# Pre-norm gain: from broadcast rows to the transposed rows, and a reordered start, in a two-layer decoder trunk

## The chip, the cores and the metric

The kernel runs on one core of a Trainium2 chip. The metric is the device time of one execution in microseconds, as the median over runs; lower is better. A core has five engines with an instruction queue each, which run in parallel and meet at semaphores: TensorE (PE in the profile; its weight loads are PEld), VectorE (DVE), ScalarE (ACT), GpSimd (POOL) and SyncE (SP), which here only issues transfers. Matmul results go to PSUM, all other tiles lie in SBUF.

## The reference

Two layers work on 512 tokens of 1024 channels. Each layer normalises x, projects it at once to 3488 columns for four head groups (low-rank attention, a gated convolution, a spatial gate, block-sparse attention), gates and concatenates their outputs, projects them back, and adds the residual. What the change touches is the first line of a layer and the first columns of the projection:

```python
def rmsnorm(x, g):
    xf = x.astype(jnp.float32)
    y = xf * lax.rsqrt(jnp.mean(xf * xf, axis=-1, keepdims=True) + EPS)
    return (y * g).astype(x.dtype)
...
    h = rmsnorm(x, norm_g)
    p = h @ w_in
    ...
    q = (rmsnorm(cq, mla_q_norm_g) @ mla_w_uq).reshape(B, S, MLA_HEADS, MLA_QK)
    kv = (rmsnorm(ckv, mla_kv_norm_g) @ mla_w_ukv).reshape(B, S, MLA_HEADS, MLA_NOPE + MLA_V)
```

## The kernel before, in words

**Tiles.** The 512 tokens are four tiles (t = 0 to 3) of 128 rows, the 1024 channels eight blocks (kt, or "k block") of 128. A float32 product is made of three matmuls of rounded values: each operand is split into hi (rounded to the matmul's type, fp32r) and lo (the rest, also fp32r), and hi·hi, hi·lo and lo·hi are summed in PSUM. `split2` makes such a pair out of a tile: ScalarE writes hi, then VectorE writes lo = source - hi.

**Pre-norm of one tile** (`pre_norm`). ScalarE squares both halves of x and sums them (`square_half`, into `xss`); POOL adds the two sums and the epsilon and takes the power -1/2 (`pow_rstd`). VectorE writes h in two halves of 512 columns, each x times the row's scalar times the gain g, where g is a row that was broadcast to all 128 partitions (`L.ng`). PE transposes each half in a group of four 128x128 blocks into one PSUM slot (`trS`, two slots, shared with cT and others); the profile calls the slot hT, and cT where the low-rank rows are transposed. One ScalarE instruction of 512 columns then writes hi (`hTh`), one of VectorE lo (`hTl`), and the slot is free.

**Where g comes from.** In layer 0 a row of g is loaded into a zeroed tile (`gz`), and two matmuls with a matrix of ones copy it to all partitions (`ng` in the profile). In layer 1 two transfers broadcast it from memory (`load_norm_gain`).

**The first stage of a layer** (`main`, `tok`). For each tile PE makes cq: eight k blocks, three matmuls of 416 columns each, from the weight units c0 to c3 (two blocks each). Then `low_chain` multiplies by the low-rank gains (ct), transposes (cT, three blocks), splits (cTh, cTl), and makes q (six matmuls of 384 columns) and kv (three of 512); `low_stats`, `q_chain` and `kv_chain` make the statistics and Q, K and Vt of the head groups. Their scalars (ms, mq, mk) are powers taken on POOL, and krt, Q and K on VectorE wait for them. The weight units are loaded by SP into raw tiles (`raw_...`) and split by `split_units`, half a unit at a time, into `whi_...` on ScalarE or VectorE and `wlo_...` on VectorE; the first units of the next product, sq, are split early, into `yTh` and `yTl`. The rope tables are about 60 small operations, most of them on POOL.

**What sets the order.** The program is written by an order of its own: each piece of work is a Python generator with a modelled time for every engine (`Order`, `Chain`), and instructions are emitted when the model says that they are due. What is emitted stays in that order on each engine, so each queue is fixed at build time, and an instruction that waits holds up all that is behind it on its engine. `ROPET` and `MIXT` are modelled times at which the rope tables and the parameter work may begin; `L0.par_t` is one for the low-rank chains; `NWARM` and `NWARM2` count matmuls on ones that run ahead of the work; `LOAD_HOOKS` say behind which weight unit a tile of x is loaded.

Of the kernel before, what the change touches and what calls it, by code (L numbers as in the profile page):

```python
# [11 lines left out]
F32 = mybir.dt.float32  # L12
F32R = mybir.dt.float32r
I32 = mybir.dt.int32
AF = mybir.ActivationFunctionType
ALU = mybir.AluOpType
AX = mybir.AxisListType

P = 128
# [15 lines left out]
NWARM, NWARM2 = 3, 1  # L35
ROPET, MIXT = 7000.0, 23000.0
# [160 lines left out]
def hybrid_trunk(ctx: ExitStack, tc: tile.TileContext, x, positions, norm_g, w_c, w_f, w_t, w_o, mla_q_norm_g,  # L197
# [180 lines left out]
    maskb = cst.tile([P, S], F32, name="maskb")  # L378
    cosT = cst.tile([P, NT, 16], F32, name="cosT")
# [94 lines left out]
    def load_norm_gain(L):  # L474
        ch = Chain(o)
        L.ng = []
        for c in (0, 512):
            g = yield from t2S.get(ch, f"ng{c}_{L.l}")
            dma(ch, P * 2048, g, dram(norm_g, L.l * D + c, [[0, P], [1, 512]]))
            L.ng.append(g)  # L480
        o.set(L.ng_ev, ch.t)

# [28 lines left out]
    for l in range(DEPTH):  # L511
        L = Layer()
        L.l = l
        L.ng_ev = Event()
        L.hT = [[Event(), Event()] for _ in range(NT)]
# [28 lines left out]
    def pre_norm(L, t, xx, t0, release):  # L544
        ch = Chain(o, t0)
        s1 = L.xss[t]
        yield from ch.pool(G.tensor_scalar, s1[:, 2:3], s1[:, 0:1], s1[:, 1:2], EPS, op0=ALU.add, op1=ALU.add)
        yield from pow_rstd(ch, s1[:, 3:4], s1[:, 2:3], 1)
        yield from ch.wait(L.ng_ev)
# [3 lines left out]
        for c in range(2):  # L553
            sl = slice(c * 512, (c + 1) * 512)
            yield from ch.dve(V.scalar_tensor_tensor, h[:, sl], in0=xx[:, sl], scalar=s1[:, 3:4], in1=L.ng[c],
                              op0=ALU.mult, op1=ALU.mult)
            tps.append(ch.t)
        release(ch)
        if t == NT - 1:
            for _ in range(2):  # L560
                (t2S if L.l else sS).put(ch)

        def half(c):
            c2 = Chain(o, tps[c])
            tp = yield from trS.get(c2, f"hT{t}_{c}_{L.l}")
            for k in range(4):
# [3 lines left out]
            yield from split2(c2, hTh[:, c * 4:c * 4 + 4, t * P:(t + 1) * P],  # L570
                              hTl[:, c * 4:c * 4 + 4, t * P:(t + 1) * P], tp.rearrange("p (k n) -> p k n", k=4))
            trS.put(c2)
            o.set(L.hT[t][c], c2.t)
# [592 lines left out]
    def main():  # L1166
        m = Chain(o)

        def tok(L, n, width, t, dst, us):

            for k in range(KT):
                if n == "c" and k % 4 == 0:
                    yield from m.wait(L.hT[t][k // 4])
# [14 lines left out]
        for L in layers:  # L1188
# [40 lines left out]
            for half in range(2):  # L1229
# [17 lines left out]
                for group, cut in (((0, 1, 2), YCUT), ((3,), 0)) if half == 0 else (((t,), 0) for t in range(NT)):  # L1247
# [16 lines left out]
                    if half == 0 and group[0] == 0 and l + 1 < DEPTH:  # L1264
                        o.spawn(load_norm_gain(layers[l + 1]))
# [9 lines left out]
    def start():  # L1275
        cw = Chain(o)
        ones = (yield from zzS.get(cw, "ones"))
        gz = yield from hS.get(cw, "gz")
        yield from cw.dve_fast(V.memset, ones[:, 0:256], 1.0)
        yield from cw.dve_fast(V.memset, gz, 0.0)  # L1280
# [4 lines left out]
        L0.ng = []  # L1285
        for c in range(2):
            L0.ng.append((yield from sS.get(cg, f"ng{c}")))
# [95 lines left out]
```

## Time and profile before

| | |
|---|---|
| median of 3 runs | 508.67 us (508.65 to 508.96) |
| the profiled execution | 508.65 us |
| its span | 506.8 us (1.85 us lie around it) |
| TensorE busy | 498.1 us, 98% |
| VectorE busy | 349.3 us, 69% |
| ScalarE busy | 296.5 us, 58% |
| GpSimd busy | 139.2 us, 27% |
| mean granted TensorE clock | 0.996 |

A row of a timeline gives start and duration in microseconds, engine, line of the kernel, operation, output<-inputs by the program's names, shape and count, and in brackets the idle time of the engine just before it with the instruction that ended it. A row of a group gives the total busy time in microseconds, the mean of one in nanoseconds, and the engine's idle time before it. Nearly all instructions go through one helper line (L158, and L184 on PE), so they are told apart by the names of the tiles. Durations overlap: an engine may start an instruction before the one ahead has ended.

### The profile page before, as it was taken

How to read it: one execution, taken by the hardware profiler on the slowest of the kernel's cores; microseconds unless marked ns; L12 is line 12 of the kernel's file. 1: busy time of each engine (PE TensorE's matmuls, PEld its weight loads, DVE VectorE, ACT ScalarE, POOL GpSimd, SP SyncE). 2: the span in 40 equal slices, each digit the busy share in tenths (PEclk: the TensorE clock that was granted, in tenths of full speed). 3: DMA queues.
4: the chain of work that ended last, by engine and by line, in shares of the span. 5: the costliest groups of instructions: out<-in, count | busy, mean ns of one | idle time of the engine just before them, and what ended most of it. 6: DMA issues, size and time to landing. Idle time of an engine off the chain costs nothing.

```text
span 506.8 us, 7665 instructions
## 1 busy us (share of the span) xinstructions
PE 498.1 (98%) x2508; PEld 423.3 (84%) x2508; DVE 349.3 (69%) x917; ACT 296.5 (58%) x891; POOL 139.2 (27%) x321
## 2 busy tenths in 40 slices
PE   6999999999999999999999999999999999999997
PEld 4898888888888888888889988888888888888886
DVE  4877975468799887635576988777868887635311
ACT  5698764567687775424247894677766777432100
POOL 6867875452000000000121488513330000000000
PEclk9999999999999999999999999999999999999999
DMA  8533415112114123464443242140142121624111
GB/s 273 165 123 114 125 43 166 41 43 66 60 43 166 52 74 109 142 175 117 143 155 126 83 125 71 55 124 2 42 167 82 43 83 49 201 84 164 66 54 50
DMA packets 20618, 51.57 MB, mean 102 GB/s; under 512 B 5985, under 2 KB 7265, under 8 KB 20578
## 3 DMA queue, kind: packets, MB, share of 16 engines
q1 hardware_dynamic: 20546, 51.08, 31.1%
q8 instruction: 20, 0.33, 0.3%
q0 software_dynamic: 32, 0.00, 0.1%
q14 instruction: 20, 0.16, 0.1%
HBM read 46.87 MB, written 4.19 MB: 101 GB/s over the span
## 4 chain that ended last, share of the span: by engine, by line
PE 90%; POOL 4%; DVE 2%; DMA 2%; ACT 1%; issue 1%; POOLq 0%; DVEq 0%
PE o L184 17%; PE kv L184 10%; PE cq L184 6%; PE sq L184 5%; PE cc L184 4%; PE gb L184 4%; PE cb L184 4%; PE gd L184 4%; PE gc L184 4%; PE ch L184 4%; PE su L184 4%; PE sa L184 3%; PE ga L184 3%; PE oa L184 2%; PE od L184 2%; PE sd L184 2%
## 5 line engine op out<-in xcount | busy, mean ns | idle before, releaser
L158 DVE TENSOR_TENSOR xr<-o,xr 128x512 f32<-128x512 f32 (+1 forms) x17 | 11.2, 658 | 42.0 <-PE o L184 42.0
L184 PE MATMUL o<-whi_wo,yTl 128*128 128x512 f32 (+1 forms) x102 | 38.4, 377 | 0.0
L184 PE MATMUL o<-wlo_wo,yTh 128*128 128x512 f32 (+1 forms) x102 | 38.4, 377 | 0.0
L184 PE MATMUL o<-whi_wo,yTh 128*128 128x512 f32 (+1 forms) x102 | 38.4, 376 | 0.0
L158 ACT ACTIVATE whi_wo<-raw_wo 128x512 fp32r<-128x512 f32 x31 | 18.3, 624 | 21.7 <-PE o L184 13.6
L158 ACT ACTIVATE pa<-pa,mna 128x256 f32<-128x256 f32 (+3 forms) x44 | 23.4, 539 | 5.2 <-DVE mna L158 5.1
L184 PE MATMUL kv<-whi_kv,hTh 128*128 128x512 f32 x64 | 26.0, 406 | 0.0
L184 PE MATMUL o<-whi_wo,yD 128*128 128x512 f32 (+1 forms) x68 | 25.7, 381 | 0.0
L158 ACT ACTIVATE pd<-pd,mnd 128x256 f32<-128x256 f32 (+3 forms) x46 | 24.5, 546 | 2.0 <-DVE mnd L158 1.5
L158 ACT ACTIVATE pha<-pTa 128x512 fp32r<-128x512 f32 (+3 forms) x32 | 13.9, 434 | 20.1 <-PE pTa L184 19.9
L184 PE MATMUL kv<-whi_kv,hTl 128*128 128x512 f32 x64 | 25.1, 392 | 0.0
L184 PE MATMUL kv<-wlo_kv,hTh 128*128 128x512 f32 x64 | 24.9, 390 | 0.0
L158 ACT ACTIVATE phd<-pTd 128x512 fp32r<-128x512 f32 (+3 forms) x32 | 13.9, 435 | 18.4 <-PE pTd L184 18.3
L184 PE MATMUL cq<-whi_c,hTh 128*128 128x416 f32 x64 | 24.3, 380 | 0.0
L184 PE MATMUL cq<-whi_c,hTl 128*128 128x416 f32 x64 | 23.3, 365 | 0.0
L184 PE MATMUL cq<-wlo_c,hTh 128*128 128x416 f32 x64 | 23.0, 360 | 0.0
L158 DVE TENSOR_TENSOR wlo_wo<-raw_wo,whi_wo 128x512 fp32r<-128x512 f32 x32 | 21.0, 687 | 2.4 <-ACT whi_wo L158 2.0
L184 PEld LDWEIGHTS o<-wlo_wo,yTh 128*128 128x128 f32 x102 | 19.2, 188 | 3.6
L184 PEld LDWEIGHTS o<-whi_wo,yTh 128*128 128x128 f32 x102 | 19.2, 188 | 3.6
L184 PEld LDWEIGHTS o<-whi_wo,yTl 128*128 128x128 f32 x102 | 19.2, 188 | 3.5
L158 DVE CUSTOM_DVE_ANT_0 pa<-sa,maskb 128x512 f32<-128x512 f32 (+3 forms) x32 | 15.0, 485 | 8.7 <-PE pTa L184 4.6
L158 DVE TENSOR_TENSOR pld<-pTd,phd 128x512 fp32r<-128x512 f32 (+3 forms) x32 | 15.5, 486 | 4.9 <-ACT phd L158 4.8
(328 smaller groups left out, 1712.8 us busy)
## 6 DMA issues: line engine op xcount, KB each, us to landing
raw_wo<-in_w_o_dram SPq DMA_DIRECT2D x16, 512.0 KB, 3.9
raw_sq<-in_w_t_dram SPq DMA_DIRECT2D x8, 512.0 KB, 3.5
raw_kv<-in_w_t_dram SPq DMA_DIRECT2D x8, 512.0 KB, 3.5
raw_c<-in_w_c_dram SPq DMA_DIRECT2D x8, 416.0 KB, 4.2
raw_ga<-in_w_f_dram SPq DMA_DIRECT2D x4, 512.0 KB, 3.6
raw_su<-in_w_f_dram SPq DMA_DIRECT2D x4, 512.0 KB, 3.5
raw_gc<-in_w_f_dram SPq DMA_DIRECT2D x4, 512.0 KB, 3.6
raw_ch<-in_w_f_dram SPq DMA_DIRECT2D x4, 512.0 KB, 3.4
```

The costliest lines, as they stand in the source:

```text
L158: f(*a, **k)
L184: f(*a, **k)
```

## The change

The gain is no longer multiplied into h. It is loaded once for both layers as 16 rows of 128 (a row for each layer and k block), transposed by PE to `gT`, in which column kt has the gain of that block's 128 channels, one per partition. h is x times the row's scalar alone (a `tensor_scalar`). After the transposes, where channels lie on partitions, hi and lo of each 128x128 block are formed with that column as a per-partition scalar: four ScalarE and four VectorE instructions of 128 columns for each half, in place of one and one of 512. PE waits for each k block (`L.hT[t][k]`), and the PSUM slot is given back after the fourth lo. `gz` with its memset, the two broadcast matmuls and the two broadcast loads of layer 1 go.

At the start, tile 0's x is loaded as 640 and 384 columns (`X0CUT`) in place of two halves; VectorE squares and sums the first part with one instruction that also adds the epsilon, ScalarE the second. Six warm-up matmuls stand ahead and none behind. x1 is loaded behind c1 and not behind c0. The rope tables are due at 13000 instead of 7000, the parameter work at 21000 instead of 23000, the low-rank chains at 15500 instead of 17500. The order of all queues in the first 45 us follows from these.

```diff
@@ -32,8 +32,8 @@
 NRAW, NW, NT2 = 2, 6, 9
 WSLACK = 0.0
 AHEAD = 4
-NWARM, NWARM2 = 3, 1
-ROPET, MIXT = 7000.0, 23000.0
+NWARM, X0CUT = 6, 640
+ROPET, MIXT = 13000.0, 21000.0
 ROPEB, ROPEV = 400.0, 200.0
 EARLY = ('sq0', 'sq1', 'sq2')
 YORDER, YCUT = (2, 3, 0, 1, 4, 6, 5, 7), 6
@@ -376,6 +376,7 @@
     ident = cst.tile([P, P], F32, name="ident")
     make_identity(nc, ident)
     maskb = cst.tile([P, S], F32, name="maskb")
+    gT = cst.tile([P, DEPTH * KT], F32, name="gT")
     cosT = cst.tile([P, NT, 16], F32, name="cosT")
     sinT = cst.tile([P, NT, 16], F32, name="sinT")
     hTh = big.tile([P, KT, S], F32R, name="hTh")
@@ -471,15 +472,6 @@
     class Layer:
         pass
 
-    def load_norm_gain(L):
-        ch = Chain(o)
-        L.ng = []
-        for c in (0, 512):
-            g = yield from t2S.get(ch, f"ng{c}_{L.l}")
-            dma(ch, P * 2048, g, dram(norm_g, L.l * D + c, [[0, P], [1, 512]]))
-            L.ng.append(g)
-        o.set(L.ng_ev, ch.t)
-
     def load_params(L):
         l = L.l
         L.cg = lay.tile([P, 384], F32, tag="cg_b", name="cg_b")
@@ -511,8 +503,7 @@
     for l in range(DEPTH):
         L = Layer()
         L.l = l
-        L.ng_ev = Event()
-        L.hT = [[Event(), Event()] for _ in range(NT)]
+        L.hT = [[Event() for _ in range(KT)] for _ in range(NT)]
         L.xss = [cst.tile([P, 4], F32, name=f"xss{t}_{l}") for t in range(NT)]
         L.qd = [Event() for _ in range(NT)]
         L.kd = [Event() for _ in range(NT)]
@@ -542,23 +533,22 @@
                           accum_out=L.xss[t][:, c:c + 1])
 
     def pre_norm(L, t, xx, t0, release):
+
         ch = Chain(o, t0)
         s1 = L.xss[t]
-        yield from ch.pool(G.tensor_scalar, s1[:, 2:3], s1[:, 0:1], s1[:, 1:2], EPS, op0=ALU.add, op1=ALU.add)
+        if L.l == 0 and t == 0:
+            yield from ch.pool(G.tensor_tensor, s1[:, 2:3], s1[:, 0:1], s1[:, 1:2], op=ALU.add)
+        else:
+            yield from ch.pool(G.tensor_scalar, s1[:, 2:3], s1[:, 0:1], s1[:, 1:2], EPS, op0=ALU.add, op1=ALU.add)
         yield from pow_rstd(ch, s1[:, 3:4], s1[:, 2:3], 1)
-        yield from ch.wait(L.ng_ev)
         h = yield from hS.get(ch, f"h{t}_{L.l}")
         hput = shared(hS, 2)
         tps = []
         for c in range(2):
             sl = slice(c * 512, (c + 1) * 512)
-            yield from ch.dve(V.scalar_tensor_tensor, h[:, sl], in0=xx[:, sl], scalar=s1[:, 3:4], in1=L.ng[c],
-                              op0=ALU.mult, op1=ALU.mult)
+            yield from ch.dve_fast(V.tensor_scalar, h[:, sl], xx[:, sl], s1[:, 3:4], None, op0=ALU.mult)
             tps.append(ch.t)
         release(ch)
-        if t == NT - 1:
-            for _ in range(2):
-                (t2S if L.l else sS).put(ch)
 
         def half(c):
             c2 = Chain(o, tps[c])
@@ -567,10 +557,17 @@
                 kt = c * 4 + k
                 yield from c2.pe(109.0, PE.transpose, tp[:, k * P:(k + 1) * P], h[:, kt * P:(kt + 1) * P], ident)
             hput(c2)
-            yield from split2(c2, hTh[:, c * 4:c * 4 + 4, t * P:(t + 1) * P],
-                              hTl[:, c * 4:c * 4 + 4, t * P:(t + 1) * P], tp.rearrange("p (k n) -> p k n", k=4))
-            trS.put(c2)
-            o.set(L.hT[t][c], c2.t)
+            ca, cv = Chain(o, c2.t), Chain(o, c2.t)
+            for k in range(4):
+                kt = c * 4 + k
+                src, g = tp[:, k * P:(k + 1) * P], gT[:, L.l * KT + kt:L.l * KT + kt + 1]
+                hi, lo = (z[:, kt, t * P:(t + 1) * P] for z in (hTh, hTl))
+                yield from ca.act(A.activation, hi, src, AF.Copy, scale=g)
+                cv.t = max(cv.t, ca.t)
+                yield from cv.dve(V.scalar_tensor_tensor, lo, in0=src, scalar=g, in1=hi.bitcast(F32), op0=ALU.mult,
+                                  op1=ALU.subtract)
+                o.set(L.hT[t][kt], cv.t)
+            trS.put(cv)
         for c in range(2):
             o.spawn(half(c))
 
@@ -1169,8 +1166,8 @@
         def tok(L, n, width, t, dst, us):
 
             for k in range(KT):
-                if n == "c" and k % 4 == 0:
-                    yield from m.wait(L.hT[t][k // 4])
+                if n == "c":
+                    yield from m.wait(L.hT[t][k])
                 if t == 0 and k % 2 == 0:
                     us.append((yield from unit(m, f"{n}{k // 2}_{L.l}")))
                 wh, wlo = us[k // 2]
@@ -1262,7 +1259,6 @@
                             if i1 == KT:
                                 o.spawn(out_chain(L, half, t, acc[t], o.now + PELAT))
                     if half == 0 and group[0] == 0 and l + 1 < DEPTH:
-                        o.spawn(load_norm_gain(layers[l + 1]))
                         load_params(layers[l + 1])
             early_put(m)
             ydS.put(m)
@@ -1275,22 +1271,18 @@
     def start():
         cw = Chain(o)
         ones = (yield from zzS.get(cw, "ones"))
-        gz = yield from hS.get(cw, "gz")
+        gn = ones[0:DEPTH * KT, 256:384]
         yield from cw.dve_fast(V.memset, ones[:, 0:256], 1.0)
-        yield from cw.dve_fast(V.memset, gz, 0.0)
         wp = yield from accS.get(cw, "warm")
         for _ in range(NWARM):
             PE.matmul(wp[:, 0:256], ones[:, 0:P], ones[:, 0:256], start=True, stop=True)
         cg = Chain(o)
-        L0.ng = []
-        for c in range(2):
-            L0.ng.append((yield from sS.get(cg, f"ng{c}")))
         x0 = yield from v4S.get(cg, "x0_0", [P, D], F32)
         L0.x[0] = x0
-        for c in range(2):
-            dma(cg, P * 2048, x0[:, c * 512:(c + 1) * 512], x[0, 0:P, c * 512:(c + 1) * 512])
+        for c, sl in enumerate((slice(0, X0CUT), slice(X0CUT, D))):
+            dma(cg, P * 4 * (sl.stop - sl.start), x0[:, sl], x[0, 0:P, sl])
             o.set(L0.x0[c], cg.t)
-        nc.sync.dma_start(gz[0:1, :], dram(norm_g, 0, [[D, 1], [1, D]]))
+        nc.sync.dma_start(gn, dram(norm_g, 0, [[P, DEPTH * KT], [1, P]]))
 
         def after(t):
             def f():
@@ -1298,10 +1290,10 @@
             return f
         for n in ("c0_0", "c1_0"):
             units[n].wanted = True
-        LOAD_HOOKS["c0_0"] = (after(1),)
+        LOAD_HOOKS["c1_0"] = (after(1),)
         LOAD_HOOKS["c3_0"] = (after(2), after(3))
         LOAD_HOOKS["ukv_0"] = (lambda: load_params(L0),)
-        L0.par_t = 17500.0
+        L0.par_t = 15500.0
         o.spawn(load_units(), None, 4)
         o.spawn(split_units(), None, 5)
         o.spawn(rope_tables(), ROPET, 6)
@@ -1309,24 +1301,29 @@
         for t in range(NT):
             def pre(t):
                 ch = Chain(o)
-                h = None
-                for c in range(2):
-                    yield from ch.wait(L0.x0[c] if t == 0 else L0.xr[t])
-                    if c == 0:
-                        h = yield from sS.get(ch, f"sq{t}")
-                    yield from square_half(ch, L0, t, c, h, L0.x[t])
+                sq = yield from sS.get(ch, f"sq{t}")
+                if t == 0:
+                    yield from ch.wait(L0.x0[0])
+                    xa, xb, s1 = x0[:, 0:X0CUT], x0[:, X0CUT:D], L0.xss[0]
+                    jk = yield from hS.get(ch, "sqj")
+                    yield from ch.dve(V.tensor_tensor_reduce, out=jk[:, 0:X0CUT], in0=xa, in1=xa, scale=1.0 / D,
+                                      scalar=EPS, op0=ALU.mult, op1=ALU.add, accum_out=s1[:, 0:1])
+                    hS.put(ch)
+                    ch = Chain(o, L0.x0[1].t)
+                    yield from ch.act(A.activation, sq[:, 0:D - X0CUT], xb, AF.Square, scale=D ** -0.5,
+                                      accum_out=s1[:, 1:2])
+                else:
+                    yield from ch.wait(L0.xr[t])
+                    for c in range(2):
+                        yield from square_half(ch, L0, t, c, sq, L0.x[t])
                 sS.put(ch)
                 yield from pre_norm(L0, t, L0.x[t], ch.t, v4S.put)
             o.spawn(pre(t), None, 0 if t == 0 else 6)
-        for c in range(2):
-            ch = Chain(o, 4000.0)
-            yield from ch.pe(860.0, PE.matmul, L0.ng[c], ones[:, 0:P], gz[:, c * 512:(c + 1) * 512], start=True, stop=True)
-        for _ in range(NWARM2):
-            PE.matmul(wp[:, 0:256], ones[:, 0:P], ones[:, 0:256], start=True, stop=True)
+        ch = Chain(o, 4000.0)
+        yield from ch.pe(60.0, PE.transpose, wp[:, 256:256 + DEPTH * KT], gn, ident[0:DEPTH * KT, 0:DEPTH * KT])
+        yield from ch.dve(V.tensor_copy, gT, wp[:, 256:256 + DEPTH * KT])
         accS.put(ch)
         zzS.put(ch)
-        hS.put(ch)
-        o.set(L0.ng_ev, ch.t)
 
     o.spawn(start())
     o.run()
```

## The prediction

> **What bounds the kernel now.** I read the page's head, then the windows by stage, the waits, the timeline of the first 40 us, and the groups by form for prices.
>
> ```profile
> span 506.8 us, 7665 instructions
> PE 498.1 (98%) x2508; PEld 423.3 (84%) x2508; DVE 349.3 (69%) x917; ACT 296.5 (58%) x891; POOL 139.2 (27%) x321
> PE   6999999999999999999999999999999999999997
> PE 90%; POOL 4%; DVE 2%; DMA 2%; ACT 1%; issue 1%; POOLq 0%; DVEq 0%
> ```
>
> TensorE (PE) is busy in every slice but the first and the last, and 90% of the chain that ended last. The stages are told apart by windows (busy time and count for PE, PEld, DVE, ACT, POOL; then granted clock):
>
> ```profile
> core 0: us, PE busy (x) PEld busy (x) DVE busy (x) ACT busy (x) POOL busy (x), PEclk, DMA share, GB/s
> 0.00:11.05 11.05, 6.51 (x19) 3.87 (x20) 4.42 (x9) 4.85 (x10) 7.34 (x36) 1.00 0.78 251
> 11.05:15.10 4.05, 4.05 (x15) 3.58 (x14) 3.57 (x7) 3.65 (x10) 3.54 (x8) 0.58 1.03 407
> 15.10:40.00 24.90, 24.30 (x141) 22.91 (x141) 20.00 (x48) 19.72 (x72) 18.89 (x38) 1.00 0.41 123
> ...
> 60.00:500.00 440.00, 439.95 (x2220) 372.97 (x2220) 303.68 (x793) 250.65 (x715) 93.81 (x219) 1.00 0.29 95
> ```
>
> From 15 to 500 us PE idles 0.6 us. So only the start can give time back, at most the few us before TensorE is dense, while any later wait of PE is a pure loss. From 15 to 40 us VectorE (DVE) is busy 20.0 of 24.9 us and PE hardly waits: there VectorE is close behind, and the change adds to it there.
>
> ```profile
> PE hT L184 <- DVE h L158: 3.0, 2, 2.6
> ```
>
> **The change, part by part.** *The start.* Rows of before:
>
> ```profile
> 1.36 0.91 DVE L158 MEMSET gz<- 128x1024 f32 x1 [0.16 <-issue]
> 4.42 2.10 PE L184 MATMUL ng<-gz,ones 128*128 128x512 f32 x4 [0.24 <-DMA gz<-in_norm_g_dram]
> 7.78 0.39 DVE L158 CAST whi_c<-raw_c 128x416 fp32r<-128x416 f32 x1 [5.50 <-DMA raw_c<-in_w_c_dram]
> 9.51 0.66 PE L184 MATMUL hT<-ident,h 128*128 128x128 f32 x4 [2.55 <-DVE h L158]
> ```
>
> The memset of gz goes, and with it the wait of the norm-gain load on SP ahead of raw_c0: raw_c0 may land up to 0.9 earlier, 6.9 to 7.8; I take 7.6, near the row, since the transfers ahead of it are the same. The two broadcast matmuls (2.1 us) and a warm-up go, three warm-ups and one 16-row transpose of g come; all lie in PE time that waits for h: nothing. One copy of g (16 columns) and the first tile's square of 640 columns on VectorE lie before raw_c0, where VectorE idles 5.50: nothing. The layer-1 gain loads leave SP in the dense part: nothing. x1 is issued behind c1 instead of ahead of it; its pre-norm stands behind weight splits on VectorE anyway.
>
> What the start then costs is VectorE's queue, in the built order, at these prices:
>
> ```profile
> L158 DVE TENSOR_TENSOR hTl<-hT,hTh 128x512 fp32r<-128x512 f32 x16 | 10.9, 684 | 5.0 <-ACT hTh L158 5.0
> L158 DVE SCALAR_TENSOR_TENSOR h<-x,xss,ng 128x512 f32<-128x512 f32 x8 | 5.9, 742 | 2.2 <-POOL xss L158 2.2
> L158 DVE TENSOR_TENSOR wlo_c<-raw_c,whi_c 128x416 fp32r<-128x416 f32 x16 | 9.1, 596 | 1.6 <-ACT whi_c L158 1.6
> L158 DVE TENSOR_TENSOR yTl<-raw_sq,yTh 128x512 fp32r<-128x512 f32 x12 | 8.3, 689 | 2.0 <-ACT yTh L158 1.9
> L158 DVE TENSOR_SCALAR pa<-pa,mna 128x512 f32<-128x512 f32 x8 | 3.9, 484 | 0.1
> L158 DVE SCALAR_TENSOR_TENSOR Vt<-kv,ms,Vt 128x256 fp32r<-128x256 f32 x8 | 3.8, 477 | 0.8 <-ACT Vt L158 0.8
> L158 DVE TENSOR_TENSOR Mt<-kv,Mt 128x256 fp32r<-128x256 f32 x8 | 3.4, 422 | 3.9 <-ACT Mt L158 3.9
> L158 DVE TENSOR_TENSOR pld<-pTd,phd 128x128 fp32r<-128x128 f32 x8 | 2.3, 286 | 0.8 <-ACT phd L158 0.8
> L158 DVE SCALAR_TENSOR_TENSOR Q<-Q,mq,gq_b 128x96 f32<-128x96 f32 x32 | 10.0, 313 | 0.5 <-POOL mq L158 0.5
> L158 DVE CAST whi_sq<-raw_sq 128x512 fp32r<-128x512 f32 x2 | 0.8, 423 | 0.0
> L158 ACT ACTIVATE phd<-pTd 128x128 fp32r<-128x128 f32 x8 | 2.2, 269 | 3.1 <-PE pTd L184 3.1
> ```
>
> A half of h falls from 742 ns to that of a scalar multiply, 484. A lo of 128 columns: 286 without a per-partition scalar (pld); the scalar adds 477 − 422 = 55 (Vt against Mt), so 344, and four of them take the place of one of 684. Back to back, starts are closer than durations:
>
> ```profile
> 22.17 0.74 DVE L158 SCALAR_TENSOR_TENSOR h<-x,xss,ng 128x512 f32<-128x512 f32 x1
> 22.83 0.42 DVE L158 TENSOR_TENSOR wlo_ukv<-raw_ukv,whi_ukv 128x256 fp32r<-128x256 f32 x1
> 23.17 0.55 DVE L158 TENSOR_TENSOR cTl<-cT,cTh 128x384 fp32r<-128x384 f32 x1
> ```
>
> that is, duration less 0.08. So a half costs 0.40 + 4 × 0.265 = 1.46 instead of 0.66 + 0.60 = 1.26. From raw_c0's landing to tile 1's last lo the queue holds 7 halves of h (2.8), 16 lo's (4.2), 8 wlo_c (4.1), four casts at 0.3 (1.2), four operations of 384 columns (1.9) and two wlo_ukv (0.7): 14.9. With 0.5 for waits, an estimate, tile 1's last lo ends at 7.6 + 14.9 + 0.5 = 23.0; cTl, just ahead of it, at 22.75.
>
> By the Trainium skill, "VectorE: DVE Perf Modes", section "The TRN2 errata — SBUF-src ops pay a fixed extra latency per instruction", cost is a fixed part per instruction plus the columns, so small tiles lose: it speaks against four for one, and the rows agree (286 for 128 columns, 684 for 512). Its figure for a PSUM source, 120 cycles plus the columns at 0.96 GHz, would make a lo 258 ns; by it the total would be about 2.0 lower (23 × 0.086).
>
> *Tile 2.* Rows at which before's PE passes the same work:
>
> ```profile
> 28.79 0.60 PE L184 MATMUL hT<-ident,h 128*128 128x128 f32 x4
> 29.15 0.44 PE L184 MATMUL cq<-whi_c,hTh 128*128 128x416 f32 x1
> ...
> 35.95 0.35 PE L184 MATMUL cq<-whi_c,hTh 128*128 128x416 f32 x1
> ```
>
> A group of four transposes takes 0.36. The 6.80 between the two cq rows (tile 2's and tile 3's fourth k block) hold 24 cq, 6 q, 3 kv and one group: 6.44 / 33 = 0.195 a matmul. In the built order both transpose groups of tile 2 stand on PE behind q0's four last matmuls, which need cTl, and kv0's three: the first group starts at 22.75 + 7 × 0.195 = 24.1 and ends 0.6 later, and the first hi on ScalarE takes about 0.35 (phd's 269 and a scalar's fetch): 25.1. VectorE comes to tile 2's first lo at 23.0 + 0.4 (h) + 0.2 (ms) = 23.6 and waits 1.5, with everything behind it. Then up to the first half's fourth lo stand 7 lo's (1.9; the halves are interleaved), three yTl (1.8), two 512-column casts (0.7), wsl (0.6, as yTl), ct (0.5), Vt (0.4), krt and ms (0.3): 6.2, end at 31.3. PE, from 22.75, has 19 matmuls (3.7) and two groups (0.7) until then, and is free at 27.2. Next stands tile 3's first transpose group. Two PSUM slots serve all of them, and a slot is now held until its half's fourth lo, not until one lo: the group can't go before 31.3 either, and the fourth k block starts at 31.3 + 0.36 = 31.7. Before starts it at 29.15, less cT1 (three transposes, about 0.25), which the new order has later: 28.9. So here the kernel is 31.7 − 28.9 = **2.8 late**.
>
> *Tile 3.* From there to its fourth lo: eight lo's (2.1), three yTl (1.8), three Q (0.7), ct 0.5, ms, mq, mk 0.6, krt and K 0.4: 6.1, end at 37.4. Before is there at 35.95, less q1 and kv1, which now come later (9 × 0.195 = 1.75): 34.2. So **3.2 late**, 0.4 more. After it the rest of tile 3 has PE's q1, kv1 and q2 between, so VectorE catches up.
>
> *POOL.* The rope tables start behind tile 1's gain instead of at once:
>
> ```profile
> 11.22 0.19 ACT L158 ACTIVATION_READ_ACCUMULATOR sq<-x 128x1 f32 x1
> ...
> 7.30 0.19 POOL L158 CAST posf<-posi 128x4 f32<-128x4 int32 x1 [1.30 <-DMA posi<-in_positions_dram]
> ...
> 26.08 0.72 POOL L158 TENSOR_TENSOR ms<-ms,nhalf 128x2 f32<-128x2 f32 x1
> ```
> ```profile
> L158 POOL TENSOR_SCALAR rope_scratch<-rope_scratch 128x64 f32<-128x64 f32 x30 | 14.3, 478 | 2.3
> L158 POOL TENSOR_TENSOR rope_scratch<-rope_scratch 128x64 f32<-128x64 f32 x22 | 9.4, 425 | 1.4
> L158 POOL TENSOR_TENSOR mq<-mq,nhalf 128x4 f32<-128x4 f32 x8 | 8.7, 1082 | 12.7 <-DVE mq L158 10.1 <-DVE ms L158 2.7
> ```
>
> Before has x1's squares at 11.4; behind one more load of 416 KB (1.05 at the 407 GB/s of the second window) and with the gain's sum and pow (about 1.0) posf comes at 13.4. To the pow of ms stand 10 and 4 rope operations of 64 columns (0.57 and 0.5 with a gap of 0.09), four short ones (1.8), tile 2's and 3's gains and three small jobs: 14.9, so 28.3; krt on VectorE asks at about 27.2. Then 7 and 6 rope operations and the pow of mq: 36.4; the first Q on VectorE asks at 33.7, and 3.9 of its queue follow to tile 3's fourth lo, 40.3 instead of 37.4. So POOL costs 0 (where its operations run quicker or VectorE asks later than I have it) to 2.9, by the groups' means; POOL's durations spread widely, and I take the middle, **1.4**.
>
> *Layer 1.* The same split, with room:
>
> ```profile
> 248.66 0.68 DVE L158 TENSOR_TENSOR hTl<-hT,hTh 128x512 fp32r<-128x512 f32 x1
> ...
> 260.36 0.43 PE L184 MATMUL cq<-whi_c,hTh 128*128 128x416 f32 x1
> ```
>
> Tile 0's last lo is 11 us ahead of its use: nothing; without that cover 0.2 a half. ScalarE's four hi's for one cost it about 0.4 a half; it is 79% busy at the start and its work runs ahead of VectorE's.
>
> Sum: 508.65 + 3.2 + 1.4 = 513.3 (506.8 of span and 1.85 around it, which stays). The profiled execution took 508.65, the median of the runs is 508.67: the same.
>
> **The rivals.** *Faster:* PE doesn't wait. VectorE keeps ahead as it does in 15–40 us of before, and what is left is the earlier start: PE free at 27.2 where before is at 28.55 (28.9 without that group): −1.3, 507.35. It decides if tile 2's fourth lo ends 4.1 earlier than I have it. For it: VectorE has 4.9 us idle in that window. Against: 1.5 of wait for transposes and yTl, wsl and casts in front. *No difference:* that lo at 28.5, and POOL in time: 508.65. *POOL never late:* 511.9. *POOL wholly late:* 514.8. *The clock:* PE would idle 4.1 us between 25 and 31.3. In before, its wait of 2.55 (row at 9.51) is followed by 4.05 us at a granted 0.58: 3.4 at half rate, 1.7 lost. Were that to come again: 515.0. By the Trainium skill, "TensorE: Matmul & The Clock Gate", section "Part 1: The HAM clock gate", an idle window of about 3.4 us halves the rate until a busy window has passed; the 3.4 us of before agree. Against it, the new idle time is cut by matmuls.
>
> **How the numbers follow.** Chances: forecast 0.25, POOL never late 0.24, wholly late 0.20, clock 0.10, faster 0.15, no difference 0.06. Without the scalar's 55 ns a lo, 23 lo's are 1.3 cheaper (512.0); with half of Vt's 477 and a full gap, 0.40 each, 3.1 dearer (516.4). The likeliest one's own range is 511.9 to 514.8; the range is 508.0 to 516.4, which leaves out "faster" and a little above. A measurement tells 0.2% from no change, 1.0 us: faster 0.15, same 0.06, slower 0.79.
>
> **What would show it.** Of the changed kernel: tile 1's last hTl near 23, the first hTl of tile 2 near 25 with VectorE idle before it (released by ScalarE's hTh), PE waiting for DVE hTl between 25 and 38 for some 4 us, POOL's pow of ms after krt's turn, hTl at 344 and h at 484, the windows from 60 us on unchanged, and VectorE over 90% busy from 7.6 to 23. If PE shows no wait in 25–40, I am wrong in the queue's length; if it waits longer, in POOL or in the clock.

## The result, and the profile after

The changed kernel takes 520.21 us (median of 4 runs, 519.78 to 520.74); the kernel before takes 508.81 in the same comparison. The ratio is 1.0221, with a 95% interval of 1.0203 to 1.0239: 11.4 us slower. The forecast was slower, at 513.3 in a range up to 516.4: the sign is right, the size is not.

The profiled execution took 520.15 us, with a span of 518.4. The page of the changed kernel:

```profile
span 518.4 us, 7722 instructions
PE 504.0 (97%) x2509; PEld 426.4 (82%) x2509; DVE 354.6 (68%) x978; ACT 301.7 (58%) x932; POOL 137.9 (27%) x314
PE   6969999999999999999999999999999999999997
PEclk8879999999999999999999999999999999999999
PE 85%; DVE 5%; ACT 4%; POOL 2%; DMA 2%; issue 1%; SPq 0%
```

One slice of TensorE has fallen from 9 to 6, the third (26 to 39 us), and there the granted clock is 7. VectorE and ScalarE have 5 us more work each, out of 518: no engine has become the bound. The windows by stage (columns as in the prediction):

```profile
0.00:11.05 11.05, 6.64 (x19) 4.92 (x20) 3.84 (x10) 3.58 (x7) 3.86 (x28) 0.91 0.79 252
11.05:15.10 4.05, 4.05 (x15) 3.87 (x13) 3.18 (x11) 3.87 (x13) 1.35 (x3) 0.50 1.00 402
15.10:25.00 9.90, 9.21 (x49) 7.83 (x47) 9.04 (x25) 7.53 (x29) 8.89 (x18) 0.96 0.46 108
25.00:30.00 5.00, 4.30 (x24) 3.47 (x24) 3.20 (x12) 3.04 (x9) 3.50 (x9) 1.00 0.56 193
30.00:40.00 10.00, 6.41 (x22) 5.28 (x23) 7.92 (x26) 7.85 (x37) 8.73 (x18) 0.66 0.33 106
60.00:500.00 440.00, 438.48 (x2199) 370.03 (x2198) 312.31 (x850) 261.35 (x775) 99.19 (x219) 1.00 0.29 94
```

The stretch from 25 to 40 us, of before and then of the changed kernel:

```profile
25.00:40.00 15.00, 15.00 (x88) 14.30 (x87) 11.82 (x30) 13.38 (x51) 10.45 (x20) 1.00 0.40 139
25.00:40.00 15.00, 10.72 (x45) 8.74 (x46) 11.12 (x38) 10.89 (x44) 12.23 (x26) 0.77 0.41 135
```

PE does 45 matmuls there where before does 88; from 30 to 40 us it is idle 3.6 us and the mean granted clock is 0.66. What it waited for, and the rows at which it passes the points that the prediction worked out:

```profile
PE hT L184 <- DVE hTl L158: 2.5, 2, 2.1
PE cq L184 <- DVE hTl L158: 1.7, 2, 1.3
PE mp L184 <- ACT vnh L158: 0.8, 1, 0.8
PE cT L184 <- DVE hTl L158: 0.6, 1, 0.6
```
```profile
35.12 1.11 PE L184 MATMUL hT<-ident,h 128*128 128x128 f32 x4 [2.09 <-DVE hTl L158]
35.88 0.69 PE L184 MATMUL cq<-whi_c,hTh 128*128 128x416 f32 x1
...
43.01 0.43 PE L184 MATMUL cq<-whi_c,hTh 128*128 128x416 f32 x1
```

Tile 2's fourth k block starts at 35.88, 7.0 us behind before (28.9; the forecast was 2.8), tile 3's at 43.01, 8.8 behind (34.2; the forecast was 3.2 and 1.4 for POOL). How late PE is at later points of the same work, from the start of the first ga, the first kv of the later product and the first o, is the table by which the experiments are read (the runs e1 to e16 are described below). The columns of lateness are those of each run's profiled execution, the last one is the median of its runs:

| | at ga | at kv | at o | end of span | median |
|---|---|---|---|---|---|
| before | 0 (64.81) | 0 (77.34) | 0 (214.22) | 0 (506.8) | 508.8 |
| the changed kernel | +8.9 | +10.2 | +10.2 | +11.6 | 520.2 |
| e1, the gain's move alone | +7.3 | +8.1 | +8.2 | +9.7 | 520.7 |
| e2, the start alone | -1.7 | -0.4 | -0.4 | -0.4 | 509.0 |
| e3, wide, its own order | +1.5 | +3.1 | +3.0 | +3.7 | 511.1 |
| e5, wide, the changed order | +7.5 | +8.8 | +8.8 | +9.3 | 518.1 |
| e9, pieces, e3's order | +2.5 | +3.9 | +3.9 | +7.2 | 515.8 |
| e13, the start, mp later | -1.5 | -1.7 | -1.7 | -1.7 | 507.4 |

So 8.9 of the 11.6 us are lost in the first stage, 1.3 between ga and kv (where PE waits for vnh at mp), and 1.4 from the first o to the end, which is layer 1 above all. One caution: VectorE's first cast of a weight block starts at 6.1 to 8.9 us in these eight profiles (last section), so part of a difference between two rows may be that alone.

### The profile page after: what moved, and what is told of

The parts are those of the page before. It is cut to its first block, busy times and chain, and to the rows that moved or that the text cites. A ratio compares the mean times of both kernels' runs of the same rounds, so it can differ in the third digit from the quotient of the medians.

```text
span 518.4 us, 7722 instructions
## 1 busy us (share of the span) xinstructions
PE 504.0 (97%) x2509; PEld 426.4 (82%) x2509; DVE 354.6 (68%) x978; ACT 301.7 (58%) x932; POOL 137.9 (27%) x314
## 4 chain that ended last, share of the span: by engine, by line
PE 85%; DVE 5%; ACT 4%; POOL 2%; DMA 2%; issue 1%; SPq 0%
PE o L184 17%; PE kv L184 9%; PE gd L184 4%; PE cq L184 4%; PE cc L184 4%; PE ch L184 4%; PE gc L184 4%; PE cb L184 4%; PE gb L184 4%; PE su L184 4%; PE sq L184 4%; PE ga L184 3%; PE sa L184 3%; PE oa L184 2%; PE od L184 2%; PE sd L184 2%
## 5 line engine op out<-in xcount | busy, mean ns | idle before, releaser
L158 ACT ACTIVATE hTh<-hT,gT 128x128 fp32r<-128x128 f32 x64 | 21.9, 367 | 18.2 <-PE hT L184 11.2
L158 ACT ACTIVATE pd<-pd,mnd 128x256 f32<-128x256 f32 (+3 forms) x51 | 27.4, 549 | 2.7 <-DVE mnd L158 2.6
L158 DVE SCALAR_TENSOR_TENSOR hTl<-hT,gT,hTh 128x128 fp32r<-128x128 f32 x64 | 20.7, 345 | 10.1 <-ACT hTh L158 10.0
L158 ACT ACTIVATE pa<-pa,mna 128x384 f32<-128x384 f32 (+3 forms) x46 | 24.6, 546 | 3.8 <-DVE mna L158 3.8
L184 PE MATMUL cq<-whi_c,hTh 128*128 128x416 f32 x64 | 25.5, 398 | 0.2 <-ACT hTh L158 0.2
```

The costliest lines, as they stand in the source:

```text
L158: f(*a, **k)
L184: f(*a, **k)
```

## The experiments

Executions of one kernel of this family spread by 0.5 to 3.9 us, those of before by up to 2.0 in one comparison; differences under 1 us between two variants are not read. e2, e3, e5, e7 and e13 came out inside a range that their expectation gave (e7 at its edge); e9, e12 and e16 fell between two ranges, and the other eight above the range that fitted them best.

**Which part of the change: e1 to e4.** Theory A blames the move of the gain, theory B the reordered start and due times.

e1, the kernel before with the gain's move alone (the diff's edits in pre_norm, its gT, its loads and waits; none of these):

```diff
-NWARM, NWARM2 = 3, 1
-ROPET, MIXT = 7000.0, 23000.0
+NWARM, X0CUT = 6, 640
+ROPET, MIXT = 13000.0, 21000.0
```

> The kernel before with the gain moved to the transposed rows and nothing else: its own first loads, squares, due times (rope tables 7000, parameter work 23000, low-rank chains 17500) and three warm-up matmuls ahead and one behind; the two broadcast matmuls and the zeroed tile go with the broadcast. Theory A (four hi's and four lo's for one, with the transposes' PSUM slot held until the fourth lo, are what makes PE wait at tiles 2 and 3): 515 to 520 us, PE waiting for hTl for 3 us or more between 25 and 36 us. Theory B (the reordered start and due times bring the late rope tables and the early splits of sq into VectorE's queue, and the split itself is harmless): 507 to 511 us, PE without a wait for hTl over 0.5 us.

520.7 us, ratio 1.0241 (1.0218 to 1.0263): the whole loss. PE waits for hTl 6.6 us in all, most of it here:

```profile
PE cT L184 <- DVE hTl L158: 3.1, 2, 1.9
PE hT L184 <- DVE hTl L158: 3.0, 3, 1.6
```

But it waits at other places than in the changed kernel: the longest three of these waits end at 15.4, 24.6 and 41.1 us, and between 25 and 36 us it is 1.05, where theory A expected 3 or more. The same move in another order loses a like amount elsewhere.

e2, the other half alone: those two lines, the loads, the split square, and `LOAD_HOOKS["c1_0"]` and `L0.par_t = 15500.0`, on the kernel before.

> The kernel before with the reordered start alone: x in 640 and 384 columns, tile 0's square partly on VectorE, x1 behind c1, six warm-up matmuls ahead, the three due times of the changed kernel; the gain stays a broadcast row (zeroed tile, two broadcast matmuls), hi and lo stay 512 columns wide. Theory A: 507 to 511 us, VectorE catches up as before. Theory B: 514 to 520 us, with POOL's power of ms and the splits of sq holding VectorE's queue near 28 to 35 us as in the changed kernel.

509.0 us, ratio 0.9999 (0.9990 to 1.0008): no difference. The start alone does no harm, so theory B is out.

e3, the changed kernel with 512-column instructions; the gain is left out of the computation, here and in e5:

```diff
-            for k in range(4):
-                yield from ca.act(A.activation, hi, src, AF.Copy, scale=g)
-                yield from cv.dve(V.scalar_tensor_tensor, lo, in0=src, scalar=g, ...)
+            yield from split2(c2, hTh[...], hTl[...], tp.rearrange("p (k n) -> p k n", k=4))
```

> The changed kernel with hi and lo formed by one instruction of 512 columns for each half, as before; the pre-norm gain is left out of the computation altogether (its load and transpose stay). Everything else, the start and the due times too, is the changed kernel's. Theory A: 507 to 511 us. Theory B: 515 to 520 us. If both parts are needed, something between, 511 to 515.

511.1 us, ratio 1.0049 (1.0035 to 1.0064), 9.1 us below the changed kernel. The 2.3 us that it still has over before were not followed up.

e4, the changed kernel with the three due times of before.

> The changed kernel with the three due times of before (rope tables 7000, parameter work 23000, low-rank chains 17500) and nothing else undone. Theory A: 516 to 521 us, PE still waits for hTl. Theory B: 508 to 513 us, POOL's power of ms in time for krt and the splits of sq behind tile 2's lo's. A half-rate stretch near 33 to 40 us comes only with a PE wait of about 4 us ahead of it.

523.6 us, ratio 1.0289 (1.0263 to 1.0315), slower still, and above the range of theory A too: the late due times were not the harm. Its half rate did not need the wait of about 4 us that was expected: it came behind one of 2.82 us (granted clock 0.83 from 40 to 50 us), and again from 80 to 90 us (0.83), where the longest wait is 0.95; behind one of 2.00 us, from 30 to 40 us, the clock stayed at 1.00. So the harm lies in the gain's move (theory A), though not only where A put its waits.

**The pieces, or the order: e5 and e9.** The program writes its queues from a model, so four instructions for one also move everything around them. Two runs hold one of these fixed. e5 has the changed kernel's queues, instruction by instruction, with one wide hi and lo where the first of the four stood; the model still books the time of four:

```diff
+    def plan(self, do, e, cost, f, *a, **k):
+        return self._emit(e, cost, f if do else lambda *b, **d: None, a, k)
...
+                yield from ca.plan(k == 0, "A", 93 + 0.834 * P + 93, A.activation, hi, src, AF.Copy)
+                yield from cv.plan(k == 0, "V", 68 + 61 + 1.047 * P, V.tensor_tensor, lo, src, ...)
```

> The changed kernel with every queue in its order, but where the first of a half's four hi's (four lo's) stood there is one of 512 columns, and the other three are gone; the pre-norm gain is left out of the computation. TensorE, POOL and SP have the changed kernel's order instruction by instruction. Theory A1 (the pieces themselves: the time of four for one on VectorE, and the fourth lo that sits far back in VectorE's queue among yTl, casts and wsl): 509 to 513 us, PE waiting for hTl under 1.5 us in all. Theory A2 (the order: tile 2's transposes behind q0 and kv0, the splits of sq ahead of the lo's): 516 to 520 us, PE still waits 3 us or more between 25 and 36 us.

518.05 us, ratio 1.0182 (1.0162 to 1.0202).

e9 is the converse, the four pieces in a row where e3 has the wide one, so that TensorE, POOL and SP have e3's order:

```diff
+            yield from c2.act(lambda *a, **k: four(A, hi4, tp4), hi4, tp4)
+            yield from c2.dve(lambda *a, **k: four(V, lo4, tp4, hi4.bitcast(F32)), lo4, tp4)
```

> The changed kernel, gain and all, in the order of the run with wide instructions: where that had one hi (one lo) of 512 columns, the four of 128 stand in a row. TensorE, POOL and SP have the order of the wide run (511.1 us), instruction by instruction. The run with one wide hi and lo in the changed kernel's order was 518.05 and the changed kernel is 520.2. If the order that the plan writes is the cause and the pieces only cost their own time on VectorE (0.46 us a half): 511.5 to 514 us, PE waiting for hTl or hTh under 2 us in all from 20 us on. If the pieces cost as much in any order: 517 to 521 us.

515.8 us, ratio 1.0126 (1.0111 to 1.0141). The four medians make a square ("pieces" are four instructions with the gain as their scalar, against one without it):

| | e3's order | the changed order | order costs |
|---|---|---|---|
| one of 512 columns | 511.1 | 518.05 | 6.9 |
| four of 128 | 515.8 | 520.2 | 4.4 |
| pieces cost | 4.7 | 2.2 | |

Both parts cost. Which is the larger depends on the way from e3 to the changed kernel: by e5 it is 6.9 for the order and then 2.2 for the pieces, by e9 4.7 for the pieces and then 4.4 for the order. What e5 loses to the order falls in the first stage: at ga it is 6.0 us behind e3, where e9 is 1.0 behind. What the pieces cost in e9 comes mostly in layer 1; 1.7 us of it are waits of PE's transposes for VectorE's work on the next tile (e9, bracketed):

```profile
262.96 0.66 PE L184 MATMUL hT<-ident,h 128*128 128x128 f32 x4 [0.57 <-DVE h L158]
270.87 0.66 PE L184 MATMUL hT<-ident,h 128*128 128x128 f32 x4 [0.87 <-DVE h L158]
273.92 0.55 PE L184 MATMUL cT<-ident,ct 128*128 128x128 f32 x3 [0.25 <-DVE hTl L569]
```

What the order does is seen most plainly in e5, where no pieces blur it. ScalarE, and then PE:

```profile
26.52 0.63 ACT L158 ACTIVATE yTh<-raw_sq 128x512 fp32r<-128x512 f32 x1 [5.30 <-DMA raw_sq<-in_w_t_dram]
27.06 1.07 ACT L158 ACTIVATE hTh<-hT 128x512 fp32r<-128x512 f32 x2
...
35.48 0.63 ACT L158 ACTIVATE yTh<-raw_sq 128x512 fp32r<-128x512 f32 x1 [1.11 <-DMA raw_sq<-in_w_t_dram]
...
36.26 1.06 ACT L158 ACTIVATE hTh<-hT 128x512 fp32r<-128x512 f32 x2
```
```profile
36.88 0.64 PE L187 MATMUL cq<-whi_c,hTh 128*128 128x416 f32 x1 [3.16 <-ACT hTh L158]
```

ScalarE sits 5.3 us on a split of sq whose load has not landed, with tile 2's hi behind it, and again at 35.5 ahead of tile 3's. POOL does the same on the load of sgw, with the power of ms behind it, for which krt on VectorE waits:

```profile
29.69 0.65 POOL L158 TENSOR_SCALAR_AFFINE_SELECT sgw<-sgw 128x512 f32<-128x512 f32 x1 [3.55 <-DMA sgw<-in_sg_w_dram]
30.31 0.72 POOL L158 TENSOR_TENSOR ms<-ms,nhalf 128x2 f32<-128x2 f32 x1
```

In the changed kernel the first wait of each kind is shorter, 1.78 and 1.04 us: the load of sq lands at nearly the same time (26.3 and 26.5), but ScalarE and POOL come to these instructions later.

**Parts of the order, undone one at a time: e10, e12, e14, e15, e16.** All on the changed kernel.

e10, splits of sq held back:

```diff
+            if u.name in ("sq0_0", "sq1_0", "sq2_0"):
+                yield from ch.wait(layers[0].hT[NT - 1][KT - 1])
```

> The changed kernel with the splits of the first three sq units held back in the plan until tile 3's last lo is planned; the order of TensorE stays nearly the changed kernel's (tile 2's transposes behind q0 and kv0, kv1 and q1 behind tile 3's cq). If the early splits of sq are the harm (ScalarE's yTh waits for a load of sq ahead of tile 2's and tile 3's hi, VectorE's yTl and casts stand among the lo's): 511 to 515 us, PE waiting for hTl under 2 us. If it is TensorE's own order, or krt behind POOL's power of ms: 517 to 521 us, waits as in the changed kernel. PE may wait instead for yTl at the first sq matmul near 45 us: up to 2 us.

522.1 us, ratio 1.0251 (1.0238 to 1.0264): nothing gained. New waits come at the sq matmuls, and a wait of 2.5 us for hTl stays at tile 3's transposes, which wait for the slot that tile 2 holds:

```profile
PE hT L184 <- DVE hTl L158: 2.9, 2, 2.5
PE sq L184 <- DVE yTl L158: 1.4, 2, 1.2
PE sq L184 <- DVE wlo_sq L158: 1.2, 2, 0.8
```

e12, a third slot for the transposes, taken from those of q and kv:

```diff
-    accS, trS, sS = psum_slots("acc", 3), psum_slots("tr", 2), psum_slots("s", 3)
+    accS, trS, sS = psum_slots("acc", 3), psum_slots("tr", 3), psum_slots("s", 2)
```

> The changed kernel with three PSUM slots for the transposes instead of two (and two instead of three for q, kv, the squares and their like, since PSUM has no bank left). The plan then writes tile 2's first transposes in tile 1's cq, ahead of most of tile 1, as the kernel before has them, and half 1 behind kv0. If the slot that is held until the fourth lo is what moves the transposes back in the order and so makes most of the loss: 511 to 515 us. If the pieces' own time and the rest of the order make it: 518 to 523 us. With two slots for q and kv alone a new wait of up to 1 us can come at q1 and kv1.

517.4 us, ratio 1.0168 (1.0151 to 1.0184): 2.8 us of the 11.4 come back, net of two new waits of PE, 1.9 us for cTl ahead of q1 and 0.8 ahead of kv1.

e15 has both edits.

> The changed kernel with three PSUM slots for the transposes and with the first three sq splits held back until tile 3's last lo: the two single undoings, of which the first gave 2.8 us (517.4) and the second nothing (522.1, where the loss moved from 25-45 us to the sq matmuls at 50-60 us). If the causes in the order lie one behind the other, so that only both together show: 511 to 515 us. If they are independent: 517 to 520 us, with PE waiting for yTl and wlo_sq between 45 and 60 us.

521.9 us, ratio 1.0238 (1.0205 to 1.0272): by the median the third slot's gain is gone again, though one of the four runs took 518.8.

e14 takes away a wait that the prediction had missed. In the changed kernel each later hi of a half waits for VectorE's lo before it (by groups: hi's idle time, lo's idle time):

```profile
L158 ACT ACTIVATE hTh<-hT,gT 128x128 fp32r<-128x128 f32 x64 | 21.9, 367 | 18.2 <-PE hT L184 11.2 <-DVE hTl L158 6.9
L158 DVE SCALAR_TENSOR_TENSOR hTl<-hT,gT,hTh 128x128 fp32r<-128x128 f32 x64 | 20.7, 345 | 10.1 <-ACT hTh L158 10.0
L158 DVE TENSOR_SCALAR h<-x,xss 128x512 f32<-128x512 f32 x8 | 3.9, 493 | 1.2 <-POOL xss L158 1.2
```

e14 issues the four hi's in a row at the first one's place; the 6.9 us are then gone from ScalarE.

> The changed kernel, every queue in its order, but with the four hi's of a half in a row on ScalarE where the first of them stood; the lo's stay where they are. In the changed kernel each later hi carries a wait for VectorE's lo before it (6.9 us of ScalarE's idle time before hTh end with a hTl), so that hi and lo go in turns through two queues; here that wait is gone. If these turns are what the pieces cost beyond VectorE's own time: 517 to 519 us (the wide instruction in the same order was 518.05). If the pieces' cost is VectorE's time alone, or the spread of the lo's among other work: 519.5 to 521 us.

521.5 us, ratio 1.0239 (1.0222 to 1.0256). The turns are real, and nothing is gained without them.

e16 moves tile 2's transposes ahead of q0 and kv0 (`tr2` is set once tile 2's second group is written):

```diff
+        if t == 0 and l == 0:
+            yield from ch.wait(tr2)
         uq_h, uq_l = yield from unit(ch, f"uq_{l}")
```

> The changed kernel with q0 held in the plan until tile 2's transposes are written: on TensorE both groups now stand ahead of q0 and kv0 (nine matmuls, 1.7 us, and the wait for cTl), and the other queues follow the plan. If the transposes' place behind q0 and kv0 is what makes VectorE wait 1.7 us for tile 2's first lo, and that wait is passed on to the end: 516.5 to 518.5 us. If VectorE's queue behind it (krt and POOL's power of ms, casts, yTl, wsl, Vt) sets tile 2's fourth lo anyway: 519.5 to 521 us.

519.3 us, ratio 1.0195 (1.0173 to 1.0217): 0.9 less, too little to be read as a gain. So none of the misplacements tried carries the order's cost by itself; where one wait was taken away, the profiles show others. POOL's wait for sgw was not tried by itself, and which combination would free the stage stays open.

**The clock: e6 and e7.** e6 fills PE's wait ahead of the first h:

```diff
+        for _ in range(6):
+            PE.matmul(wp[:, 0:256], ones[:, 0:P], ones[:, 0:256], start=True, stop=True)
```

> The changed kernel with six more warm-up matmuls behind the transpose of g, which fill the stretch from 6.5 to 9.3 us in which PE waits for h. If the half rate from 9 to 16 us (two windows, one in before) costs time by itself: 1.5 us less, 518.5 to 519.0 us. If VectorE's queue sets the first 25 us anyway (PE waits for hTl and cTl at 21 and 25 us): no change, 519.7 to 520.7 us.

521.3 us, ratio 1.0246 (1.0228 to 1.0263): no gain, though the granted clock is 1.00 from 0 to 25 us.

e7 puts dummy matmuls into tile 2's waits:

```diff
+FILL = {1: 16, 2: 22}
+                        PE.matmul(spare[0][:, 416:512], hTh[:, 0, t * P:(t + 1) * P], wh[:, 0, 0:96],
+                                  start=False, stop=False)
```

> The changed kernel with 38 dummy matmuls of 96 columns in tile 2's waits (16 behind its second k block, 22 behind its third), into columns of the accumulator that nothing reads: PE stays active between 29 and 35 us. If the half rate from 33 to 40 us is a consequence of the wait and costs what its records show (4 us of work at twice the time): 1.5 to 2.5 us less, 517.7 to 518.7 us, granted clock 1.0 from 33 to 40 us. If VectorE or POOL is just as late behind PE there: 519.5 to 521 us.

521.0 us, ratio 1.0238 (1.0210 to 1.0267). In the profiled execution the clock is at full in the stretch (its window, and a wait of PE):

```profile
30.00:40.00 10.00, 9.76 (x66) 8.77 (x65) 8.56 (x28) 6.84 (x31) 8.81 (x17) 1.00 0.35 105
```
```profile
PE cT L185 <- DVE hTl L159: 1.6, 2, 1.0
```

So the half rate came with the wait. Its price is not settled. PE meets a next wait sooner, 1.6 us for hTl at cT against 0.6, and the median is no better than the changed kernel's. But the profiled execution, with a mean granted clock of 0.997, took 519.15 us, 1.0 less than the changed kernel's; the other three had 0.986 to 0.992 and took 519.83 to 522.59, so the dummies did not hold the clock in every run, or it fell elsewhere.

**The start by itself: e8, e11 and e13.** e8 is e2 with the due times of before, e11 e2 with `MIXT` at 23000.

> The kernel before with the reordered loads, tile 0's square split between VectorE and ScalarE and six warm-up matmuls, but its own due times (7000, 23000, 17500); broadcast gain and 512-column hi and lo. The reordered start alone was 509.0, with PE 1.9 us ahead at 25 us and a wait of 1.3 us at the first mp matmul near 69 us. If the due times bring that wait: 506.5 to 507.5 us. If the gain at the start is always given back at mp, because VectorE's queue there does not move with PE: 508.4 to 509.3 us.

> The kernel before with the reordered start, as in the run of 509.0, but the parameter work due at 23000 as before (rope tables 13000, low-rank chains 15500). If the wait of 1.3 us at the first mp matmul near 69 us comes from the parameter work and with it from the order in VectorE's queue: 506.5 to 507.8 us, faster than before. If it stays: 508.5 to 509.5 us.

510.9 us, ratio 1.0040 (1.0026 to 1.0053), and 510.8 us, ratio 1.0032 (1.0020 to 1.0043): both slower than e2, and outside both of their ranges. Moving a due time leaves a wait at mp (0.8 and 0.6 us) and adds another (0.6 and 0.5 us for wlo_sq). In e2 PE is 1.7 us ahead at ga, and 1.3 are lost here, 0.83 of it as idle time:

```profile
70.26 0.39 PE L184 MATMUL mp<-vnh,wsh 128*128 128x256 f32 x1 [0.83 <-ACT vnh L158]
```

e13 is e2 with the mp matmuls planned behind more of ga:

```diff
+        if l == 0:
+            ch.t += 3000.0
         for g2 in range(2):
             mp = yield from accS.get(ch, f"mp{g2}_{l}")
```

> The kernel before with the reordered start (509.0), and the first mp group planned 3 us later, so that PE does 9 matmuls of ga ahead of it. If the 1.9 us that the start gains by 25 us are lost only in the wait for vnh at mp (1.3 us at 69 us): 507.2 to 508.0 us, faster than before. If VectorE's vn chain just ends the wait elsewhere: 508.5 to 509.5 us.

507.4 us (12 runs), ratio 0.9974 (0.9965 to 0.9984): the wait is gone, the 1.7 us stay in the profile, and this is the fastest version here, by 1.3 us. It has the reordered start, the broadcast gain and the wide instructions.

## Why the prediction was wrong in size

**The bound** was read rightly: TensorE is dense, and 8.9 of 11.6 us were lost in the first stage by its waits.

**The prices** of single instructions held: a lo 345 ns (344 forecast), a half of h 493 (484). The trace agrees in kind with the rule of the Trainium skill, "VectorE: DVE Perf Modes", section "The TRN2 errata — SBUF-src ops pay a fixed extra latency per instruction", that many small tiles pay a fixed cost each: four pieces take 4 × 345 = 1380 where one took 684. The estimate by its figure for a PSUM source, 258 ns, was too low, and the sum by it further off.

**The step that failed is the sum along VectorE's queue up to tile 2's fourth lo** (31.3, hence 2.8 late). Measured rows of VectorE:

```profile
8.49 0.38 DVE L158 CAST whi_c<-raw_c 128x416 fp32r<-128x416 f32 x1 [1.83 <-DMA raw_c<-in_w_c_dram]
...
12.73 0.35 DVE L158 SCALAR_TENSOR_TENSOR hTl<-hT,gT,hTh 128x128 fp32r<-128x128 f32 x1 [0.52 <-ACT hTh L158]
...
14.99 0.48 DVE L158 TENSOR_SCALAR h<-x,xss 128x512 f32<-128x512 f32 x1 [0.35 <-POOL xss L158]
...
23.32 0.49 DVE L158 TENSOR_SCALAR h<-x,xss 128x512 f32<-128x512 f32 x1 [0.81 <-POOL xss L158]
...
25.25 0.34 DVE L158 SCALAR_TENSOR_TENSOR hTl<-hT,gT,hTh 128x128 fp32r<-128x128 f32 x1
...
27.93 0.35 DVE L158 SCALAR_TENSOR_TENSOR hTl<-hT,gT,hTh 128x128 fp32r<-128x128 f32 x1 [1.72 <-ACT hTh L158]
...
30.64 0.25 DVE L158 SCALAR_TENSOR_TENSOR krt<-krt,ms,gr_b 128x32 f32<-128x32 f32 x1 [0.72 <-POOL ms L158]
...
34.47 0.59 DVE L158 SCALAR_TENSOR_TENSOR hTl<-hT,gT,hTh 128x128 fp32r<-128x128 f32 x2
```

The end is at 35.06, 3.8 later, in four terms. raw_c0 was there at 8.5 and not 7.6: 0.9, in this execution (the last section has others). From there to tile 1's last lo the queue took 17.1 us (25.59 - 8.49) and not 15.4: 1.7. Of this 1.2 are waits, 0.52 for hTh, 0.35 and 0.81 for POOL's gains, where 0.5 was allowed for all; the other 0.5 is spread over 41 instructions. Then 2.3 and not 2.1 passed until tile 2's first lo: 0.2. From there to its fourth it took 7.1 and not 6.2: 0.9, 0.7 of it krt behind POOL's power, which the forecast had in another term. So the larger part is time in which VectorE waited for a load or another queue; the instructions' times were nearly right. A last 0.4 is PE's: at half rate its group takes 0.76 and not 0.36, and 7.0 late is 4.2 more than forecast.

The rest of the gap: 11.6 were lost and 4.6 forecast. Of the 7.0 between, 4.2 are lost here, none in tile 3 (below), 1.3 at mp and 1.4 in layer 1.

**The mechanism at this place** was right: the wait for tile 2's first lo was 1.72 (1.5 forecast), and tile 3's transposes went 0.06 us after the fourth lo, as the held slot demanded. But only part of the loss comes back with a third slot (e12). PE's waits for hTl between 25 and 38 us come to 3.7, close to the "some 4" of the forecast's sign; that is luck, since 2.09 of them are at tile 3's transposes and 1.65 at tile 2's k blocks, where none was forecast.

**Tile 3 and the clock.** Between the two points 1.8 us were added, just the sum of 0.4 and 1.4 that was forecast for VectorE and POOL, but by luck: no wait of PE stands between them, and they came as half rate. A granted 0.66 in 30 to 40 us is 6.8 us at half rate. The rival on the clock thus came true in the records. The rule of "TensorE: Matmul & The Clock Gate", section "Part 1: The HAM clock gate", in the Trainium skill, with its window of about 3.4 us, agrees in the length, which is two such windows; but PE was not idle for a whole one, its waits of 1.34 and 2.09 us have a matmul between them. As a price, 1.7, the rival is not confirmed: e7 has full rate in its profile, 1.0 us less there, and a median that is no better.

**POOL.** The power of ms ended at 30.61 (28.3 forecast), that of mq at 38.66 (36.4):

```profile
14.91 0.19 POOL L158 CAST posf<-posi 128x4 f32<-128x4 int32 x1
...
29.27 0.65 POOL L158 TENSOR_SCALAR_AFFINE_SELECT sgw<-sgw 128x512 f32<-128x512 f32 x1 [1.04 <-DMA sgw<-in_sg_w_dram]
29.89 0.72 POOL L158 TENSOR_TENSOR ms<-ms,nhalf 128x2 f32<-128x2 f32 x1
```

That is 2.3 later than the forecast's own late case: 1.5 since the rope tables began at 14.91 and not 13.4, and the rest lies within the wait of 1.04 for sgw's load. It cost 0.7 at krt and no wait at Q, since by then VectorE was late too.

**Costed at nothing.** The forecast put the exchange of PE's first matmuls at nothing. The half-rate stretch at the start grew from 3.4 to 6.8 us (by the granted clocks of the windows up to 25 us), but without it the time is no better (e6). Two other terms were not nothing. Layer 1 was "nothing" with 11 us of room for tile 0's lo: 1.4 lost in the changed kernel and 3.3 in e9, about half of e9's at the transposes of later tiles, whose room was not looked at. The wait at mp, 1.3, was not seen at all.

**The rival "faster"** rested on the start's gain of 1.3; e2 shows such a lead at ga, 1.7, by itself, and e13 keeps 1.3 of it in the median. It was real, and swallowed.

## What to carry to other kernels

Where a program writes its queues from modelled times, a change of instruction sizes changes the order of everything, and the order can cost as much as the instructions or more: 4.4 to 6.9 us for the order here, 2.2 to 4.7 for the pieces. Build the two crossed versions, new instructions in the old order and old instructions in the new, before blaming either, and walk the square both ways. In a stage where several queues are near their limit, allow each hand-over between queues its own wait, and expect that undoing one can leave the next.

## What was not expected of the hardware

The landing of the first weight block varies from one profile to another by 1.5 us or more with the same first loads: VectorE's first cast of it starts at 8.49 us in the changed kernel, 8.91 in e10, 6.91 in e4.

```profile
6.91 0.38 DVE L158 CAST whi_c<-raw_c 128x416 fp32r<-128x416 f32 x1 [0.78 <-DMA raw_c<-in_w_c_dram]
```

Of the twelve versions with the changed kernel's first loads, nine have it at 8.40 to 8.96 us and three (e4, e5, e7) at 6.91 to 6.98; e4 is the slowest of all, so an early landing alone does not make a run fast. In e13, whose gain is loaded in the old way, it was 6.98 us, and that version's runs spread from 506.93 to 508.83 us. There is one profile of each version, so whether the landing changes from run to run of one kernel is not shown, and what decides it wasn't tried.
